# The order of the last store and the x loads of a tile on SyncE's queue, in a residual add with RMSNorm on one core

## The chip, the cores and the metric

The kernel runs on one core of one Trainium2 chip. The metric is device microseconds (us) of that core, from one execution of the whole kernel. Three runs of the kernel before took 4003.17, 4016.13 and 4017.06 us; their median, 4016.13, is the time before.

## The reference

The inputs are x and residual, both 32 x 2048 x 2048 in fp32, and gamma, 2048 numbers in fp32. Each of the 65,536 rows is treated alone:

```
z   = x + residual
rms = sqrt(mean(z ** 2, axis=-1) + eps)
out = z / rms * gamma
```

So 1073.7 MB are read and 536.9 MB are written, whatever the order of the work.

## The kernel before, in words

**Tiles.** The rows are cut into 65 tiles. Tile 0 has 3 rows in each of the 128 partitions, tiles 1 to 63 have 8, tile 64 has 5. A full tile is 8.39 MB of x, as much of residual, as much of output. The tile's x goes into one of two buffers, z[0] and z[1], by the tile's parity, and everything is done there in place: VectorE adds residual to it, scales it, and the stores read it. So the buffer that held tile i-1 takes x of tile i+1, and a load of x may begin only where the store has finished. Residual goes into one area of 9 rows (`r_area`), which neighbouring tiles share, shifted by one row: residual of tile i+1 is loaded once the first two of the three adds of tile i are done.

**Groups.** The store of a tile and the x load into the same buffer are cut into four groups, q = 0 to 3, each of every fourth partition (q, q+4, ...): 32 partitions, 2.10 MB in a full tile. Each group's store counts on a semaphore of its own (`s_out[q]`), and the x load of the same group waits for that. In this text S0 to S3 are the four stores of a tile (helper `store`, line 170) and L0 to L3 the four loads of x into the same partitions (helper `load_x`, line 149).

**Engines and queues.** SyncE (SP in the profile, SPq its DMA queue, q1) issues all stores and all loads of x, in the order of `sync_program` and `sp_turn`, which is written out by hand: one call of `sp_turn(sp, i)` for i = 1 to 63. It waits until VectorE has finished tile i-1 (semaphore `done`), stores tile i-1, and loads x of tile i+1. An instruction of SP that waits for a semaphore holds up all that stand behind it on SP. ScalarE (ACT) issues the loads of residual from its own queue (ACTq, line 161, q10), in `act_turn`, between its sums of squares. VectorE (DVE) runs `dve_turn`: it waits for all four x loads (`x_in`) and for residual (`r_in`), adds in three parts (line 195), then per half a reciprocal (line 219) and one scaling per row (line 200), the roots coming from ACT (line 256). At the end of the second half it raises `done`. TensorE does nothing.

**The turn before.** `sp_turn` queues S0, S1, S2 of tile i-1, then L0, L1, L2 of tile i+1, each after its group's store has landed, then S3, then L3, which waits until S3 has landed.

**Head and tail.** Tiles 0 and 1 are loaded whole, and gamma is spread over the partitions meanwhile. The last tiles are stored by rows (line 175): tile 63 in two halves, tile 64 in three pieces.

Of the kernel before, what the change touches and what calls it, by code (L numbers as in the profile page):

```python
# [9 lines left out]
def kernel(  # L10
# [32 lines left out]
    Q = 4  # L43
# [16 lines left out]
    def rows(t, i):  # L60
        k = sizes[i]
        return t[starts[i] : starts[i] + P * k, :].rearrange("(p r) m -> p r m", r=k)
# [82 lines left out]
    def group(q):  # L145
        return slice(q, P, Q)

    def load_x(sp, i, q):
        sp.dma_start(out=z[i % 2][group(q), : sizes[i], :], in_=rows(x_f, i)[group(q)]).then_inc(  # L149
            ev["x_in"][i % 2], U  # L150
        )
# [17 lines left out]
    def store(sp, i, q):  # L169
        sp.dma_start(out=rows(o_f, i)[group(q)], in_=z[i % 2][group(q), : sizes[i], :]).then_inc(  # L170
            s_out[q], U
        )
# [4 lines left out]
    def sp_turn(sp, i):  # L177


        def load(q):  # L180
            sp.wait_ge(s_out[q], i * U)
            load_x(sp, i + 1, q)

        Turn(i).wait(sp, "done", -1)
        for q in range(Q - 1):
            store(sp, i - 1, q)
        for q in range(Q - 1):
            load(q)
        store(sp, i - 1, Q - 1)
        load(Q - 1)  # L190


    def add(v, i, a, b):
# [92 lines left out]
    def sync_program(sp):  # L286
        whole_x(sp, 0)
        load_r(sp, Turn(0))

        sp.wait_ge(tail_ev["add"], 1)  # L290
        for q in range(4):
            sp.dma_start(  # L292
                out=stage[32 * q : 32 * q + 1],
                in_=gamma.partition_broadcast(1).rearrange("p (a b) -> p a b", a=16),
            ).then_inc(g_in, U)
        load_r(sp, Turn(1))
        whole_x(sp, 1)
        for i in range(1, last):
            sp_turn(sp, i)
        (a0, b0), (a1, b1) = halves(last - 1)  # L300
        sp.wait_ge(half, 1)
        store_rows(sp, last - 1, a0, b0)
        Turn(last).wait(sp, "done", -1)
        store_rows(sp, last - 1, a1, b1)
        for k, (a, b) in enumerate(tail):
            sp.wait_ge(tail_ev["done"], k + 1)
            store_rows(sp, last, a, b)
# [94 lines left out]
```

## Time and profile before

| | |
|---|---|
| median of three runs | 4016.13 us (4003.17 to 4017.06) |
| the profiled execution, its own time | 3982.87 us |
| its span | 3981.1 us (1.77 us lie around it) |
| DVE busy | 2300.7 us, 58% of the span |
| ACT busy | 1059.7 us, 27% |
| HBM read, written | 1073.77 MB, 536.87 MB; mean 405 GB/s over the span |

The busy time of an engine is the sum of its instructions, without the issuing of DMAs. A DMA queue's share is the time that its packets took, summed over the core's 16 DMA engines, as a share of 16 spans. In a table of stretches (windows), a packet is booked in the stretch in which it starts, with all of its time: so the DMA share of a short stretch can be above 1, and share divided by GB/s tells how long the DMA engines took per byte there. In a timeline a row's first number is its start in us from the span's start, the second its length, and in brackets stands how long the engine had been idle and what ended that. The length of a DMA instruction on SP or ACT is that of its issue, not of the transfer.

### The profile page before, as it was taken

Reading aid. Unit: us, or ns where it says so; the run is one execution under the profiler, and the core shown is the slowest. Engines: PE = TensorE matmul, PEld = TensorE weight load, DVE = VectorE, ACT = ScalarE, POOL = GpSimd, SP = SyncE. Lnnn points to the kernel's source line nnn. Section 1 sums busy time; section 2 is a strip of 40 time slices with the busy share of each in tenths; the row PEclk is TensorE's granted clock in tenths of the full one; section 3 lists DMA queues with packets and bytes.
Section 4 is the critical chain, followed back from the end, with each engine's and each line's share of the span. In section 5 each row is a group of like instructions: output and inputs, shape, how many; then the busy total and the mean of one; then the engine's idle time right before and its main releaser. Section 6 shows DMA issues by size and latency. Waiting matters only on the chain.

```text
span 3981.1 us, 4005 instructions
## 1 busy us (share of the span) xinstructions
DVE 2300.7 (58%) x842; ACT 1059.7 (27%) x1157; POOL 0.2 (0%) x4
## 2 busy tenths in 40 slices
DVE  5646556465564655646556465564655646556465
ACT  2313223132231322313223132231322313223132
POOL 0000000000000000000000000000000000000000
DMA  9999999999999999999999999999999999999999
GB/s 421 411 392 420 399 402 410 390 415 396 400 411 400 411 400 408 403 400 412 400 409 402 400 411 400 400 411 400 413 398 411 411 400 411 400 400 410 390 421 379
DMA packets 34694, 1610.73 MB, mean 405 GB/s; under 512 B 9280, under 2 KB 9344, under 8 KB 9344
## 3 DMA queue, kind: packets, MB, share of 16 engines
q1 hardware_dynamic: 25616, 1085.34, 65.9%
q10 hardware_dynamic: 9072, 525.34, 30.5%
q14 instruction: 6, 0.05, 0.0%
HBM read 1073.77 MB, written 536.87 MB: 405 GB/s over the span
## 4 chain that ended last, share of the span: by engine, by line
DMA 94%; SPq 3%; DVE 1%; issue 1%; another core or an unknown queue 1%; ACT 0%; ACTq 0%; DVEq 0%
DMA out_dram<-z 93%; SPq L170 2%; SPq L149 1%; DVE z L200 1%; DVE z L195 1%; DMA z<-in_gamma_dram 0%; DMA z<-in_x_dram 0%; ACT sq_junk L246 0%; SPq L292 0%; DVE z L311 0%; ACT rms L256 0%; DVE rstd L219 0%; ACTq L161 0%; DVE tail_rstd L329 0%
## 5 line engine op out<-in xcount | busy, mean ns | idle before, releaser
L195 DVE TENSOR_TENSOR z<-z,r_area 128x8192 f32<-128x8192 f32 (+2 forms) x192 | 1104.8, 5809 | 1589.9 <-DMA z<-in_x_dram 1579.0
L246 ACT ACTIVATE sq_junk<-z 128x2048 f32<-128x2048 f32 x512 | 962.1, 1879 | 2891.2 <-DVE z L195 2880.9
L200 DVE SCALAR_TENSOR_TENSOR z<-z,rstd,gamma_tile 128x2048 f32<-128x2048 f32 x507 | 1156.5, 2343 | 4.5
L246 ACT ACTIVATION_READ_ACCUMULATOR sq_junk<-z 128x1 f32 x512 | 95.4, 186 | 0.0
L219 DVE RECIPROCAL rstd<-rms 128x4 f32<-128x4 f32 (+1 forms) x128 | 22.3, 174 | 58.2 <-ACT rms L256 58.2
L256 ACT ACTIVATE rms<-ssq,eps_tile 128x4 f32<-128x4 f32 (+1 forms) x128 | 38.0, 297 | 11.7
L200 DVE SCALAR_TENSOR_TENSOR z<-z,tail_rstd,gamma_tile 128x2048 f32<-128x2048 f32 x5 | 11.6, 2346 | 0.1
L313 DVE LOAD_MASK_SELECT gamma_tile<-z x1 | 0.0, 14 | 16.3 <-DMA z<-in_gamma_dram 16.3
L195 DVE TENSOR_TENSOR z<-z 128x2048 f32<-128x2048 f32 x3 | 6.7, 2284 | 0.0
L313 DVE STREAM_SHUFFLE gamma_tile<-z 128x2048 f32<-128x2048 f32 x1 | 2.3, 2290 | 0.0
L311 DVE MEMSET z<- 128x2048 f32 x1 | 1.8, 1765 | 0.4 <-issue 0.4
L246 ACT ACT_TABLE_LOAD x1 | 1.3, 1283 | 0.9 <-SPq L80 0.9
L256 ACT ACT_TABLE_LOAD x1 | 1.3, 1283 | 0.1
L256 ACT ACTIVATE tail_rms<-tail_ssq,eps_tile 128x2 f32<-128x2 f32 (+1 forms) x3 | 0.9, 295 | 0.1
L310 DVE MEMSET eps_tile<- 128x1 f32 x1 | 0.1, 59 | 1.0 <-SPq L80 1.0
L329 DVE RECIPROCAL tail_rstd<-tail_rms 128x2 f32<-128x2 f32 (+1 forms) x3 | 0.5, 158 | 0.0
L383 POOL MEMSET const-bfloat16-1.0<- 128x1 bf16 x1 | 0.1, 101 | 0.0
L383 POOL MEMSET const-uint8-127<- 128x1 uint8 x1 | 0.1, 101 | 0.0
L383 POOL MEMSET const-float32-0.0<- 128x1 f32 x1 | 0.1, 98 | 0.2 <-issue 0.2
L383 POOL MEMSET const-float32-1.0<- 128x1 f32 x1 | 0.1, 98 | 0.0
## 6 DMA issues: line engine op xcount, KB each, us to landing
out_dram<-z SPq DMA_DIRECT2D x2, 4096.0 KB, 20.9
z<-in_x_dram SPq DMA_DIRECT2D x4, 1280.0 KB
r_area<-in_residual_dram ACTq DMA_DIRECT2D x1, 5120.0 KB, 25.6
out_dram<-z SPq DMA_DIRECT2D x2, 2048.0 KB, 8.6
z<-in_x_dram SPq DMA_DIRECT2D x249
out_dram<-z SPq DMA_DIRECT2D x248, 20.6
z<-in_x_dram SPq DMA_DIRECT2D x1, 3072.0 KB
z<-in_residual_dram SPq DMA_DIRECT2D x1, 3072.0 KB, 17.2
```

The lines of the kernel that those rows point to most:

```text
L149: sp.dma_start(out=z[i % 2][group(q), : sizes[i], :], in_=rows(x_f, i)[group(q)]).then_inc(ev["x_in"][i % 2], U)
L170: sp.dma_start(out=rows(o_f, i)[group(q)], in_=z[i % 2][group(q), : sizes[i], :]).then_inc(s_out[q], U)
L195: return v.tensor_add(out=s, in0=s, in1=res(i, a, b))
L200: ins = v.scalar_tensor_tensor(out=s, in0=s, scalar=rs[:, c + g - a : c + g - a + 1], in1=gamma_tile[:, :], op0=mult, op1=mult,)
L219: v.reciprocal(out=rstd[p][h][:, :n], in_=rms[p][h][:, :n]).then_inc(dve, U)
L246: s.activation(out=sq_junk[:, :], in_=src[:, g, :], func=Act.Square, accum_out=sq[:, c + g - a : c + g - a + 1],)
L256: return s.activation(out=rm, in_=sq, func=Act.Sqrt, bias=eps_tile[:, :], scale=inv_d)
L310: v.memset(eps_tile[:, :], float(eps))
L311: v.memset(stage, 0.0).then_inc(tail_ev["add"], 1)
L313: v.stream_shuffle(gamma_tile[:, :].rearrange("p (a b) -> p a b", a=16), stage, [0] * 32)
L329: v.reciprocal(out=tail_rstd[:, a:b], in_=tail_rms[:, a:b]).then_inc(dve, U)
L383: nc = _bacc.Bacc("TRN2", target_bir_lowering=False, num_devices=1)
```

## The change

Within `sp_turn`, all four stores of tile i-1 are queued first, and then the four loads of x of tile i+1, each still waiting for the store of its own group. Before, the last store stood between the loads of the third and the fourth group. No wait is added or removed, and the other engines' programs are the same, with line numbers behind the place lower by two.

```diff
         Turn(i).wait(sp, "done", -1)
-        for q in range(Q - 1):
+        for q in range(Q):
             store(sp, i - 1, q)
-        for q in range(Q - 1):
+        for q in range(Q):
             load(q)
-        store(sp, i - 1, Q - 1)
-        load(Q - 1)
```

One turn on SP in the program before, of a tile in buffer z0 (out_0_dram is the output, in_x_dram is x; x2 stands for two such instructions in a row; the last row begins the next turn, of buffer z1):

```order
L170 DMA out_0_dram<-z0 32x16384 [waits done0]
L170 DMA out_0_dram<-z0 32x16384 x2
L149 DMA z0<-in_x_dram 32x16384 [waits s_out0]
L149 DMA z0<-in_x_dram 32x16384 [waits s_out1]
L149 DMA z0<-in_x_dram 32x16384 [waits s_out2]
L170 DMA out_0_dram<-z0 32x16384
L149 DMA z0<-in_x_dram 32x16384 [waits s_out3]
L170 DMA out_0_dram<-z1 32x16384 [waits done1]
```

The sixth row is S3, directly ahead of L3, which waits for it. The same turn on SP in the changed program:

```order
L170 DMA out_0_dram<-z0 32x16384 [waits done0]
L170 DMA out_0_dram<-z0 32x16384 x3
L149 DMA z0<-in_x_dram 32x16384 [waits s_out0]
L149 DMA z0<-in_x_dram 32x16384 [waits s_out1]
L149 DMA z0<-in_x_dram 32x16384 [waits s_out2]
L149 DMA z0<-in_x_dram 32x16384 [waits s_out3]
L170 DMA out_0_dram<-z1 32x16384 [waits done1]
```

S3 has moved past the three loads L0 to L2 and past their three waits; the loads keep their order among themselves and L3 is still the last of the turn.

## The prediction

> **What bounds the kernel now.** I read the page first: its last-ended chain and the share of its DMA queues.
>
> ```profile
> span 3981.1 us, 4005 instructions
> ...
> DMA packets 34694, 1610.73 MB, mean 405 GB/s; under 512 B 9280, under 2 KB 9344, under 8 KB 9344
> ## 3 DMA queue, kind: packets, MB, share of 16 engines
> q1 hardware_dynamic: 25616, 1085.34, 65.9%
> q10 hardware_dynamic: 9072, 525.34, 30.5%
> ...
> DMA 94%; SPq 3%; DVE 1%; issue 1%; another core or an unknown queue 1%; ACT 0%; ACTq 0%; DVEq 0%
> ```
>
> The chain is DMA for 94%, so compute hides. The two queues' packets take 65.9 + 30.5 = 96.4% of the DMA engines' time, so the engines stand idle for 3.6% of 3981.1 us: 143 us, or 2.27 us in each of the 63 turns, if it falls on the turns alike. Small as that looks, it must be found: then it must be asked whether the 96.4% are all full speed.
>
> Next, SP's timeline over one turn in the middle:
>
> ```profile
> 2026.19 0.47 SPq L149 DMA_DIRECT2D z<-in_x_dram  x1
> 2026.71 1.87 SPq L170 DMA_DIRECT2D out_dram<-z  x3
> 2039.76 10.35 SPq L149 DMA_DIRECT2D z<-in_x_dram  x3
> 2050.14 0.60 SPq L170 DMA_DIRECT2D out_dram<-z  x1
> 2088.22 0.47 SPq L149 DMA_DIRECT2D z<-in_x_dram  x1
> ```
>
> The first row is L3 of a turn, issued when S3 had landed; then S0 to S2 of the next tile, L0 to L2 as each store lands, and S3 at 2050.14. L3 comes only at 2088.22, 38.1 us later, because S3 stands behind L1 and L2 and shares the engines with residual. From L3 to L3 the turn takes 62.03 us. ACT's residual load and VectorE's work in that turn, with the median time to landing of the residual loads from the DMA view as the last row:
>
> ```profile
> 2035.10 17.36 DVE L195 TENSOR_TENSOR z<-z,r_area 128x8192 f32<-128x8192 f32 x3 [25.18 <-DMA z<-in_x_dram]
> 2050.44 0.34 ACTq L161 DMA_DIRECT2D r_area<-in_residual_dram  x1
> 2053.60 9.12 DVE L200 SCALAR_TENSOR_TENSOR z<-z,rstd,gamma_tile 128x2048 f32<-128x2048 f32 x4
> 2062.85 9.12 DVE L200 SCALAR_TENSOR_TENSOR z<-z,rstd,gamma_tile 128x2048 f32<-128x2048 f32 x4
> ...
> r_area<-in_residual_dram ACTq DMA_DIRECT2D x62, 37.9
> ```
>
> Residual, issued at 2050.44, lands about 37.9 us later, at 2088.3: in the same moment as S3. So when S3 lands, nothing else is queued anywhere: not residual, not x, and not the next tile's stores, which have been ready since 2062.85 + 9.12 = 2071.97 but stand behind L3 on SP. Both queues run dry once per turn. The table of stretches shows it, with two stretches of the head for comparison (the last two numbers of a row are DMA share and GB/s):
>
> ```profile
> 30.00:52.00 22.00, 5.68 (x4) 2.04 (x3) 0.00 (x0) 1.00 1.00 432
> 62.10:72.90 10.80, 10.80 (x2) 6.01 (x6) 0.00 (x0) 1.00 1.09 467
> 2023.70:2027.40 3.70, 0.00 (x0) 0.00 (x0) 0.00 (x0) 1.00 0.00 0
> 2027.40:2033.80 6.40, 0.00 (x0) 0.00 (x0) 0.00 (x0) 1.00 1.03 328
> 2033.80:2048.40 14.60, 13.30 (x2) 4.43 (x5) 0.00 (x0) 1.00 1.00 431
> 2048.40:2085.80 37.40, 22.58 (x12) 12.08 (x14) 0.00 (x0) 1.00 1.04 449
> ```
>
> Third row: for 3.7 us no packet starts; L3's begin 1.2 us after its issue. Fourth row: L3 alone. Its packets take 1.03/328 = 0.00314 of the engines' time per GB/s, against 1.00/432 = 0.00231 in the head: 1.36 times as long. Fifth and sixth: S0 to S2 alone, then the loads and S3 beside residual, at 1.00/431 and 1.04/449, full speed again. So a turn loses twice: an empty queue, and a first load behind it that runs slowly.
>
> **The change part by part.** It moves one instruction per turn, S3, in 63 turns, with its 2.10 MB, on SP and on q1, past the three loads L0 to L2 and their waits. It is not moved past anything of ACT's queue, and VectorE's and ACT's programs are untouched. Bytes and issue times are the same: S3's 0.60 us is paid right behind S2's, while q1 has work.
>
> What it removes. S3 runs directly behind S2, and lands about one group's time (2.10 MB at 432 GB/s: 4.85 us) after it. Then L3 is issued while L0 to L2 are still queued. SP then waits for `done`. In the quoted turn, counted from the add's start at 2035.10 (x complete), S0 to S3 end about 4 x 4.85 = 19.4 us later, and so L3 is issued at about +20 us; VectorE finishes the tile at +36.9 (2071.97 - 2035.10). At +36.9 the next four stores go into q1, behind what is left of L0 to L3, which ends with the turn at about +58. So 21 us of cover stand between the stores' issue and an empty q1. If that cover were gone, each us of lateness would cost one us per turn.
>
> What a turn then costs. It moves 3 x 8.39 = 25.17 MB. At 432 GB/s, the head's rate, that is 58.25 us. What it takes now is read from the adds: the second tile's, then the first and last of 61 that follow each other, and the last tile's:
>
> ```profile
> 105.76 17.36 DVE L195 TENSOR_TENSOR z<-z,r_area 128x8192 f32<-128x8192 f32 x3 [10.96 <-DMA r_area<-in_residual_dram]
> ...
> 168.17 17.36 DVE L195 TENSOR_TENSOR z<-z,r_area 128x8192 f32<-128x8192 f32 x3 [25.53 <-DMA z<-in_x_dram]
> ...
> 3900.40 17.36 DVE L195 TENSOR_TENSOR z<-z,r_area 128x8192 f32<-128x8192 f32 x3 [25.59 <-DMA z<-in_x_dram]
> ...
> 3948.35 10.96 DVE L195 TENSOR_TENSOR z<-z,r_area 128x4096 f32<-128x4096 f32 x3 [12.04 <-DMA z<-in_x_dram]
> ```
>
> (3900.40 - 168.17) / 60 = 62.20 us per turn. So 62.20 - 58.25 = 3.95 us per turn can go. The two losses account for it: L3 alone takes 0.36 x 4.85 = 1.73 us too long, the empty queue the remaining 2.2, which agrees with the 2.27 of the page.
>
> The sum. 60 turns x 3.95 = 237 us. The last turn goes from 3900.40 to 3948.35 in 47.95 us and moves 8.39 + 2 x 5.24 = 18.87 MB, 43.7 us at 432 GB/s: 4.3 us more. The turn from 105.76 to 168.17 (62.41 us) is like the sixty: 4 us. The one ahead of it I take at nothing: its stores are those of the small tile 0, and its end waits for residual (first row), not for x. Behind the last add nothing changes: 3981.1 - 3948.35 = 32.75 us, set by the adds, roots and scalings of tile 64 and their stores, while tile 63's stores run beside them. So the span falls by 245 us to 3736. As a check, all 1610.73 MB at 432 GB/s are 3729 us, and a few us of head and tail come on top.
>
> Not all will go. The mean turn is 62.20 where the quoted one is 62.03; what makes some turns longer by 0.17 on the mean I can't place, so I keep it: 62 x 0.17 = 11 us. Another unknown is the change from load to store: in the quoted turn L3 is the only load directly ahead of a store without residual beside it, and it is slow. That a load behind others, with no empty queue ahead, is fast is shown by the second row: L0 to L2 of the second turn, groups of 32 partitions and no residual yet, at 1.09/467 = 0.00233. The bounds are 0 and 1.73 us per turn; I take 0, being nearest to that row. Span 3736 + 11 = 3747, own time 3747 + 1.8 = 3749 us.
>
> The median of the three runs is 33 us (0.8%) above the profiled execution. If this stretches every turn alike, the new median is 3749 x 1.0083 = 3780; if it lies in the empty queues and slow loads, it goes with them and 3749 stays. I take the middle, **3764 us**, with 3730 to 3795 as this case's own range.
>
> The rate 432 GB/s carries the sum. The Trainium skill (DMA: Bandwidth & Descriptors, Bandwidth: Measured) gives 425 GB/s for a 16 MB load by one core. By that figure a turn would take 59.2 us, an estimate, and the median would come out near 3825; this case's own rows hold 432 over 22 us, so they decide.
>
> Who is late next? Residual: issued 15.3 us after the add begins (2050.44 - 2035.10), landing 37.9 later, at +53.2, against +58 for x: 5 us of slack. It shares the engines with three groups, as before (L1, L2, S3 then; L0 to L2 now), so I leave 37.9. VectorE's chain of 36.9 us fits in 58.
>
> **The rivals.**
>
> *L3 stays slow.* Perhaps not the empty queue makes it slow, but what it is: the last group, alone, with a store behind it. All that would still hold. Then only the 2.2 us of emptiness go, and 62 x 1.73 = 107 us come back: own time 3856, median 3856 to 3888. Against it stands the second row of the stretches; for it, that every slow L3 has a store behind it and that row's loads mostly a load. A load of a group reads rows 256 KB apart, in all DMA engines at once. The Trainium skill (DMA: Bandwidth & Descriptors, Latency and other measured facts) reports DMA copies at 207 GB/s where the rows of the partitions lie 512 KiB apart, and infers that streams in step meet in the same memory channel; by that L3 is slow by its addresses wherever it stands in step. The trace agrees only where a queue starts empty: 328 GB/s at 1.03 there, full speed with the same addresses at 62.1. I give 0.17.
>
> *The gap moves.* The queues could run dry somewhere else: if S0 to S3 were queued only after L3 had ended, the empty time would come back between L3 and S0, and the time would stay within 20 us of 4016. By the rows `done` comes 21 us before that; it would need VectorE's 36.9 us to become 58. Chance 0.04.
>
> *Slower: residual beside loads only.* In the new order residual runs beside L0 to L2, three loads; before, beside L1, L2 and S3. If reading alone from both queues slowed the engines, the 8.39 + 3 x 2.10 = 14.7 MB, 34 us at full speed, would stretch. From 12% on (3.95/34) the gain is gone; at L3's 1.36 times it is 12.2 us per turn, 8.3 net, and the median 4016 + 62 x 8.3 = 4530. Against it: the sixth row, where residual and loads share for most of 37 us, at full speed (1.04/449 = 0.00232), and the first, loads alone. Chance 0.04.
>
> **How the numbers follow.** The forecast has the remaining 0.75. A measurement of this kernel can tell about 0.5%, 20 us, from no change. Faster: 0.75 + 0.17 = 0.92; within 0.5%: 0.04; slower: 0.04. The range starts at 3728 (all bytes at 432 GB/s) and must go into the first rival to leave out no more than 2 in 10: to 3872, the middle of its 3856 to 3888.
>
> **What would show it.** Right: both DMA queues together near 99% of the engines' time, mean near 430 GB/s; add to add 58.3 to 58.6 us; in SP's timeline four stores in a row some 37 us after the add begins and L3 20 us after it, no row in which SP waits 38 us for a store; no stretch of 3 us without packets, and L3's stretch at a share over GB/s of 0.0023. If that quotient is 0.0031 there and the turn 60, the first rival is right. Wrong: a turn of 62 us with a new empty stretch, or adds that end their wait on residual rather than on x.

## The result, and the profile after

The changed kernel takes 3732.51 us (median of four runs, 3732.22 to 3733.14), the kernel before 4010.93 us (four runs, the three from above among them, 4003.17 to 4017.06). The ratio is 0.9307, with a 95% interval of 0.9287 to 0.9327: 7% faster.

The page of the changed kernel, the rows that answer to those of before:

```profile
span 3730.9 us, 4005 instructions
...
DMA packets 34695, 1610.73 MB, mean 432 GB/s; under 512 B 9281, under 2 KB 9345, under 8 KB 9345
## 3 DMA queue, kind: packets, MB, share of 16 engines
q1 hardware_dynamic: 25616, 1085.34, 67.3%
q10 hardware_dynamic: 9072, 525.34, 32.6%
...
DMA 65%; DVE 27%; issue 5%; SPq 1%; ACT 1%; another core or an unknown queue 1%; ACTq 0%; DVEq 0%
```

The DMA engines are now at work for 67.3 + 32.6 = 99.9% of the span. Two products tell where the time went. Work: 0.964 x 3981.1 = 3838 us before, 0.999 x 3730.9 = 3727 us now, for the same bytes, so the packets took 111 us less. Idleness: 143 us before, 4 us now, 139 us less. Together 250 us, the whole difference of the spans. The chain of waits now runs through VectorE for 27% of the span, and that is a trap for a reader: stores wait for `done` and the chain follows that wait, but while SP waits there, the queue still holds loads. An engine that stands in the chain is not yet a bound; the DMA engines' 99.9% say what is.

SP's timeline over one turn, then VectorE's add and ACT's residual load of the same turn, and the two adds that bound sixty turns with the last tile's add behind:

```profile
1944.51 2.42 SPq L170 DMA_DIRECT2D out_dram<-z  x4
1970.49 17.48 SPq L149 DMA_DIRECT2D z<-in_x_dram  x4
2002.68 2.41 SPq L170 DMA_DIRECT2D out_dram<-z  x4
...
1965.79 17.36 DVE L193 TENSOR_TENSOR z<-z,r_area 128x8192 f32<-128x8192 f32 x3 [21.30 <-DMA z<-in_x_dram]
1981.12 0.34 ACTq L161 DMA_DIRECT2D r_area<-in_residual_dram  x1
...
164.31 17.36 DVE L193 TENSOR_TENSOR z<-z,r_area 128x8192 f32<-128x8192 f32 x3 [17.30 <-DMA z<-in_x_dram]
...
3653.80 17.36 DVE L193 TENSOR_TENSOR z<-z,r_area 128x8192 f32<-128x8192 f32 x3 [21.38 <-DMA z<-in_x_dram]
...
3698.09 10.96 DVE L193 TENSOR_TENSOR z<-z,r_area 128x4096 f32<-128x4096 f32 x3 [8.39 <-DMA z<-in_x_dram]
```

The four stores go out at 2002.68, 36.9 us after the add began; the last of the four loads at 1970.49 + 17.48 = 1987.97, 22.2 us after it. A turn takes (3653.80 - 164.31) / 60 = 58.16 us, against 62.20. The table of stretches shows what became of the gap and of L3; the middle row holds L3, between residual's end and the next stores:

```profile
1928.00:1957.00 29.00, 16.45 (x9) 6.03 (x7) 0.00 (x0) 1.00 1.00 434
1957.00:1963.00 6.00, 0.00 (x0) 0.00 (x0) 0.00 (x0) 1.00 0.91 393
1963.00:1984.00 21.00, 17.36 (x3) 8.34 (x10) 0.00 (x0) 1.00 1.02 443
```

There is no stretch without packets, and L3 runs at 0.91/393 = 0.0023, where it stood at 0.0031.

### The profile page after: what moved, and what is told of

Read it like the earlier page. It is cut to its first block, busy times and chain, and to the rows that moved or that the text cites. A ratio compares the mean times of both kernels' runs of the same rounds, so it can differ in the third digit from the quotient of the medians.

```text
span 3730.9 us, 4005 instructions
## 1 busy us (share of the span) xinstructions
DVE 2300.7 (62%) x842; ACT 1059.7 (28%) x1157; POOL 0.2 (0%) x4
## 3 DMA queue, kind: packets, MB, share of 16 engines
q1 hardware_dynamic: 25616, 1085.34, 67.3%
q10 hardware_dynamic: 9072, 525.34, 32.6%
## 4 chain that ended last, share of the span: by engine, by line
DMA 65%; DVE 27%; issue 5%; SPq 1%; ACT 1%; another core or an unknown queue 1%; ACTq 0%; DVEq 0%
DMA out_dram<-z 33%; DMA z<-in_x_dram 30%; DVE z L193 13%; DVE z L198 13%; SPq L170 1%; DMA r_area<-in_residual_dram 1%; ACT sq_junk L244 0%; DMA z<-in_gamma_dram 0%; ACTq L161 0%; DVE rstd L217 0%; ACT rms L254 0%; DVEq L314 0%; DVEq L139 0%; SPq L290 0%
```

## The experiments

The theory on trial: a turn lost time only because both queues ran empty when S3 landed, and because what follows such a gap starts slowly. The rival that was left: it is S3's place that counts, what runs beside residual, or what stands beside what. All kernels compute the whole output. From each profile I work out, as above, the idle time of the DMA engines (span less busy) and the excess of the packets (busy less the 3727 us of the changed kernel); a share has one decimal, so both are good to some 4 us. The profiled execution can lie above the median of its runs, by 10 us with stores and loads in turn and by 8 with S3 one load earlier. Each ratio is to runs of the kernel before beside those of the row (medians 3999 to 4011 us); small differences between rows are best read from the ratios.

| kernel | median us | ratio to before (95%) | idle us | excess us |
|---|---|---|---|---|
| before (profile) | 4010.93 | 1 | 143 | 111 |
| changed | 3732.51 | 0.9307 (0.9287 to 0.9327) | 4 | 0 |
| S3 one load earlier | 3742.12 | 0.9354 (0.9338 to 0.9369) | 0 | 21 |
| order of before, L3 from ACT | 3745.78 | 0.9362 (0.9344 to 0.9380) | 4 | 12 |
| gap ahead of the stores | 3896.86 | 0.9744 (0.9728 to 0.9761) | 113 | 55 |
| gap between loads | 3974.44 | 0.9930 (0.9913 to 0.9946) | 143 | 106 |
| wait for S3, residual queued | 3835.46 | 0.9587 (0.9564 to 0.9609) | 19 | 86 |
| wait for S2, residual queued | 3783.60 | 0.9446 (0.9426 to 0.9466) | 4 | 55 |
| stores and loads in turn | 3818.92 | 0.9539 (0.9523 to 0.9555) | 4 | 97 |
| L0 alone between stores | 3841.30 | 0.9590 (0.9574 to 0.9606) | 12 | 105 |
| two groups, order of before | 4296.35 (one run) | | 253 | 314 |

**How much of the move is needed.** S3 is moved past one load only.

```diff
         for q in range(Q - 1):
             store(sp, i - 1, q)
-        for q in range(Q - 1):
+        for q in range(Q - 2):
             load(q)
         store(sp, i - 1, Q - 1)
-        load(Q - 1)
+        for q in range(Q - 2, Q):
+            load(q)
```

> S3 is moved past one load only: S0 S1 S2 L0 L1 S3 L2 L3. Theory (a turn loses time only where both queues are empty, and then by the slow load behind the gap): when S3 lands, L2 is still queued, so nothing runs empty and the time is that of the changed kernel, 3732 us, within 15. Rival (what pays is that S3 no longer runs beside residual, in favour of a load): S3 still runs beside residual, so 3950 to 4011. A middle time, 3800 to 3900, would say that one group of 2.1 MB is too little cover.

3742.12 us: as the theory had it. S3 still runs beside residual, and nearly all of the gain is there. One group queued behind S3 is cover enough to keep the queues from running empty. What is left to the changed kernel, 10 us between the medians, is excess of the packets (21 us in the profiled execution), not idleness.

**The order of before, without SP being held up.** S3 stays behind L2, and L3 still waits for it, but on ScalarE's queue, after the turn's last root.

```diff
         store(sp, i - 1, Q - 1)
-        load(Q - 1)
...
         inc(root(s, chain, ssq[p][1][:, :n], rms[p][1][:, :n]), "rms_b", i)
+        if i:
+            s.wait_ge(s_out[Q - 1], i * U if t.it is None else t.it * U + i * U)
+            src = rows(x_f, i + 1) if t.it is None else x_full[t.it + i]
+            s.dma_start(
+                out=z[(i + 1) % 2][group(Q - 1), : sizes[i + 1], :], in_=src[group(Q - 1)]
+            ).then_inc(ev["x_in"][(i + 1) % 2], U)
```

> The order of before, S3 as late as there and L3 still waiting for it, but L3 is issued from ScalarE's queue at the end of its turn, so that SP goes on to the next tile's stores as soon as they are ready. Theory: when S3 lands, S0 to S2 of the next tile are queued, the engines never run empty: 3732 to 3770 us (some turns longer, since L3 now shares with S0 and x is complete up to 5 us later). Rival (the place of S3 itself matters, behind the loads and beside residual): 4011.

3745.78 us. So the place of S3 is not the cause. What cost the time was that L3's wait for S3 kept the next tile's finished stores, which stand behind it on SP, out of the queue. SP's waits (us in total, times, longest) show it. Before:

```profile
SPq L149 <- DMA out_dram<-z: 3612.7, 252, 38.2
SPq L170 <- DVE z L200: 33.6, 2, 30.1
```

With L3 issued from ScalarE, where the stores' line is L172, and then the queues of this kernel's page:

```profile
SPq L172 <- DVE z L201: 1892.3, 63, 31.3
...
q1 hardware_dynamic: 22592, 954.00, 59.1%
q10 hardware_dynamic: 12096, 656.68, 40.8%
```

Before, SP came late to the stores in all but two cases, since the tile was finished when it arrived there. Now it waits for VectorE in every turn, so the stores go out as soon as they can, and the DMA engines are at work for 99.9% of the span.

**The gap given back, ahead of stores.** The changed kernel with one more wait: the stores are queued only when x of the running tile has landed.

```diff
+        Turn(i).wait(sp, "x_in")
         Turn(i).wait(sp, "done", -1)
         for q in range(Q):
             store(sp, i - 1, q)
```

> The changed kernel with one more wait: SP queues S0 to S3 only when x of the running tile has landed, so both queues are empty once per turn, ahead of a store instead of a load. Theory: the empty time comes back, 63 x 2.2 = 139, but not the slow load, since a store stands behind the gap: 3871 us, and S0's stretch at a share over GB/s of 0.0023. If whatever stands first behind a gap is slow, 63 x 3.95 = 249 comes back: 3981, S0 at 0.0031. If emptiness costs nothing and only S3's place counts: 3732.

3896.86 us, 26 us more than the theory's 3871 and far from the other two. The idle time comes back, 113 us or 1.8 per turn. The table of stretches of this kernel, from the gap to residual's start:

```profile
1987.60:1990.10 2.50, 0.00 (x0) 0.00 (x0) 0.00 (x0) 1.00 0.00 0
1990.10:2006.60 16.50, 16.04 (x3) 6.26 (x7) 0.00 (x0) 1.00 1.03 445
2006.60:2009.00 2.40, 1.48 (x2) 2.31 (x4) 0.00 (x0) 1.00 1.32 437
```

Stores behind a gap are at full speed at once (1.03/445 = 0.0023). But an excess of 55 us, 0.9 per turn, appears where nobody had looked for it: in the third row, the last packets of S3, directly ahead of residual's load, at 1.32/437 = 0.0030.

**The gap given back, between loads.** L3 is issued only when L0 to L2 have landed, which is when residual lands too.

```diff
-        for q in range(Q):
+        for q in range(Q - 1):
             load(q)
+        sp.wait_ge(ev["x_in"][(i + 1) % 2], Turn(i).at(1, Q * U) - U)
+        load(Q - 1)
```

> The changed kernel with one more wait: L3 is issued only when L0 to L2 have landed, which is when residual lands too, so both queues run empty once per turn as in the kernel before, and L3 stands alone behind the gap, but behind loads and not behind a store. Theory A (a load behind an empty queue is slow): gap and both of L3's packets come back, 63 x 3.95, about 3981 us, L3's first packets at 3.2 us against 2.4. Theory B (only the change between storing and loading, in step, is slow): gap and the packet ahead of the next store come back, 63 x (2.2 + 1.0), about 3930 us.

3974.44 us: theory A, within 7 us. Idle time and excess are those of the kernel before (143 and 106 us, against 143 and 111), though no store has anything to do with this gap. The queues of its page, and its stretches (gap, L3, the stores behind it):

```profile
q1 hardware_dynamic: 25616, 1085.34, 65.9%
q10 hardware_dynamic: 9072, 525.34, 30.5%
...
1957.60:1961.30 3.70, 0.00 (x0) 0.00 (x0) 0.00 (x0) 1.00 0.00 0
1961.30:1966.80 5.50, 0.00 (x0) 0.00 (x0) 0.00 (x0) 1.00 1.19 381
1966.80:1988.00 21.20, 17.99 (x5) 9.07 (x10) 0.00 (x0) 1.00 1.03 445
```

L3, alone behind the gap and with stores behind it, stands at 1.19/381 = 0.0031 again.

**A wait on S3 without a gap.** SP issues the loads only when S3 has landed; residual is queued on the other queue by then.

```diff
         for q in range(Q):
             store(sp, i - 1, q)
+        sp.wait_ge(s_out[Q - 1], i * U)
         for q in range(Q):
             load(q)
```

> The changed kernel with one more wait: SP issues L0 only when S3 has landed, so q1 is empty once per turn between S3 and L0, at a time when residual has been queued for some us on the other queue. Theory (only a gap on both queues together costs): 3732 to 3750 us. Rival (every landing that the queue waits for costs its 2.2 us, or 3.95 with the slow load): 3871 or 3981.

3835.46 us: neither. One half of the theory holds: residual covers the empty SP queue, and the idle time is only 19 us in place of 143. The other half falls: 86 us of excess are there without a gap. The page and the stretches of this kernel (stores; the change to residual; residual and loads; the end of L3 with S0 behind it):

```profile
span 3832.4 us, 4068 instructions
...
q1 hardware_dynamic: 25616, 1085.34, 67.0%
q10 hardware_dynamic: 9072, 525.34, 32.5%
```

```profile
1960.00:1979.00 19.00, 15.94 (x3) 6.16 (x7) 0.00 (x0) 1.00 1.00 431
1979.00:1982.00 3.00, 2.04 (x3) 2.91 (x4) 0.00 (x0) 1.00 1.07 393
1982.50:2013.00 30.50, 17.39 (x9) 6.94 (x9) 0.00 (x0) 1.00 1.02 440
2015.50:2018.30 2.80, 0.00 (x0) 0.00 (x0) 0.00 (x0) 1.00 1.34 421
```

Full speed in the first and third (0.0023), 0.0027 where storing turns to loading, 0.0032 where loading turns to storing. Against 432 GB/s the second row lost 3.0 x (1.07 - 393/432) = 0.5 us and the fourth 2.8 x (1.34 - 421/432) = 1.0 us of this turn, so about two thirds of the excess stand at the end of L3. The slow packets need no gap.

**Which packets of a lone load are slow.** Two groups instead of four in the kernel before, so that a group has four packets per DMA engine.

```diff
-    Q = 4
+    Q = 2
```

> The order of before with two groups instead of four: S0, L0 after S0, S1, L1 after S1, four packets for each DMA engine in a group. The queue now runs empty twice per turn, ahead of L0 and of L1. Theory A (whatever load stands alone behind an empty queue is slow throughout): L1's stretch of about 13 us at a share over GB/s of 0.0031 all along, 9.6 us lost per turn, about 4340 us. Theory B (only packets next to a change between storing and loading, with the DMA engines in step, are slow): first and last quarter of L1 at 0.0031, the middle at 0.0023, 7 us lost per turn, about 4170 us.

4296.35 us in one run, nearer to A, but the stretches show B's pattern in L1, which is issued at 1974.50:

```profile
1974.80:1978.50 3.70, 0.00 (x0) 0.00 (x0) 0.00 (x0) 1.00 0.86 283
1978.50:1982.00 3.50, 0.00 (x0) 0.00 (x0) 0.00 (x0) 1.00 1.30 562
1982.00:1988.00 6.00, 0.00 (x0) 0.00 (x0) 0.00 (x0) 1.00 0.96 317
```

0.0030, 0.0023, 0.0030: the beginning, behind the gap, and the end, ahead of the stores, are slow, the middle is not. With the gap between loads this fits two causes, one for each end of L3: its first packets are slow as a load behind a gap (a gap behind loads did it too), its last because stores follow. The second is read from the place of the slow packets alone; no kernel was run in which nothing follows such a load.

**Does the order matter where nothing runs empty?** The changed kernel's stores and loads in turn, S0 S1 L0 S2 L1 S3 L2 L3:

```diff
-        for q in range(Q):
-            store(sp, i - 1, q)
-        for q in range(Q):
-            load(q)
+        store(sp, i - 1, 0)
+        for q in range(1, Q):
+            store(sp, i - 1, q)
+            load(q - 1)
+        load(Q - 1)
```

> The changed kernel's stores and loads in turn: S0 S1 L0 S2 L1 S3 L2 L3. The queue always holds at least one group when a load is issued. Theory (the order is free as long as nothing runs empty): 3732 us, within 15. If having all four stores together, far from the loads, matters in itself: over 3760.

3818.92 us, a miss: no idle time (4 us), and 97 us of excess. The stretches of this kernel, with residual running and around L0 ahead of it:

```profile
1975.00:2005.00 30.00, 17.53 (x9) 7.08 (x9) 0.00 (x0) 1.00 1.03 448
2020.30:2028.00 7.70, 7.70 (x2) 3.81 (x3) 0.00 (x0) 1.00 0.98 340
```

0.0029 around L0, 0.0023 where the other changes stand, beside residual.

**One load between stores.** L0 alone is put between S1 and S2.

```diff
-        for q in range(Q):
-            store(sp, i - 1, q)
-        for q in range(Q):
-            load(q)
+        store(sp, i - 1, 0)
+        store(sp, i - 1, 1)
+        load(0)
+        store(sp, i - 1, 2)
+        store(sp, i - 1, 3)
+        for q in range(1, Q):
+            load(q)
```

> The changed kernel with L0 alone moved between the stores: S0 S1 L0 S2 S3 L1 L2 L3. In the interleaved order the slow packets stood around L0, before residual starts, and L1 beside residual was at full speed. If a load between stores costs only while no residual runs beside it, this order costs as much as the interleaved one: about 3819 us, within 20. If the number of changes between storing and loading counts, wherever they stand, it costs about half of that: about 3775 us. If neither, 3732 us.

3841.30 us, 2 us outside the first answer's range: one load of 2.1 MB between stores costs as much as the whole order in turn. Its stretches (S0 and S1, L0 with S2, residual with the loads):

```profile
1960.00:1971.50 11.50, 5.73 (x1) 0.00 (x0) 0.00 (x0) 1.00 0.99 427
1971.50:1979.30 7.80, 7.80 (x2) 4.66 (x5) 0.00 (x0) 1.00 1.07 370
1984.00:2013.00 29.00, 18.51 (x10) 8.15 (x9) 0.00 (x0) 1.00 1.00 434
```

**A milder wait.** As the wait on S3, but on S2, with S3 still queued:

```diff
+        sp.wait_ge(s_out[Q - 2], i * U)
         for q in range(Q):
             load(q)
```

> The changed kernel with one more wait, milder than the one ahead of the loads in an earlier run (3835 us): SP issues L0 to L3 only when S2 has landed, with S3 still queued for 4.85 us. Theory (a wait on all 16 engines brings them into step, and changes between loading and storing in step are slow): with one group of cover the engines need not stop for each other, 3735 to 3780 us. If 3835 us comes back, the issue of four loads at once is slow by itself, whatever the cover.

3783.60 us, 4 us above the range given, and half-way between the changed kernel (3732.5) and the wait on S3 (3835.5). The excess is 55 us, in the change from L3 to S0:

```profile
1960.00:1988.00 28.00, 13.91 (x8) 3.52 (x5) 0.00 (x0) 1.00 1.02 440
1988.50:1993.80 5.30, 0.00 (x0) 0.00 (x0) 0.00 (x0) 1.00 1.01 383
```

0.0023 ahead of it, 0.0026 in it. The same change from L3 to S0, with no gap ahead of it, stands at 0.0023 in the changed kernel, 0.0026 here, 0.0032 with the wait on S3. How far the 16 DMA engines have drifted apart goes with it in part: in the trace's records of semaphore landings, the parts of S0 from the 16 engines land within 0.7 us (median over the turns) in the kernel before, 2.6 us in the two kernels with a wait, 6.1 us in the changed one. That fits the idea that engines in step are slow at the change. But it is a correlation, and it leaves much unexplained: the two waits differ (0.0026 and 0.0032) at the same spread, L0 between stores is slow at a spread of 3.4 us, and the stores behind a gap are fast at a spread of 0.2 us. Why a change is slow stays open.

## Why the prediction was right, and where it was not

**What bounds the kernel, and the two losses.** Right, and in size: 2.2 us of emptiness and 1.73 us of a slow L3 per turn were forecast, and 139 / 63 = 2.2 and 111 / 63 = 1.8 went. A kernel without the move (L3 from ACT) and one with the least of it (S3 one load earlier) show that it was the emptying, and two more bring the emptiness back; of these, the gap between loads brings back the slow L3 as well.

**The turn.** 58.25 us plus 0.17 kept; measured 58.16. SP's steps came as worked out: stores at +36.9 us, L3 at +22 (forecast +20). The 21 us of cover held: the stores are queued at +37, and x, the last of what stood ahead of them, is complete at +58.

**The sum.** Sixty turns gave 3732.23 - 3489.49 = 243 us (237 forecast). The last turn, 3698.09 - 3653.80 = 44.29, gave 3.7 (4.3 forecast); the end behind it is the same, 32.81 us. The first turns were misjudged. Of the kernel before, the add of tile 1; that of tile 2, at 105.76, was shown:

```profile
57.88 17.36 DVE L195 TENSOR_TENSOR z<-z,r_area 128x8192 f32<-128x8192 f32 x3 [20.84 <-DMA z<-in_x_dram]
```

The same two adds after:

```profile
58.45 17.36 DVE L193 TENSOR_TENSOR z<-z,r_area 128x8192 f32<-128x8192 f32 x3 [21.52 <-DMA z<-in_x_dram]
...
110.14 17.36 DVE L193 TENSOR_TENSOR z<-z,r_area 128x8192 f32<-128x8192 f32 x3 [14.76 <-DMA r_area<-in_residual_dram]
```

The turn that I took at nothing became 110.14 - 58.45 = 51.69 us in place of 47.88, because its end waits for residual. By the trace's packet records residual ran beside the small store S3 and L3 before; now its first packet starts 1.8 us later (78.5 us in place of 76.6), and it runs beside L3 and S0 of the next tile. The turn behind it then took 54.17 in place of 62.41. Together they gave 4.4 us, against 4 forecast: the two errors cancel.

**The 31 us that the forecast was too high.** 3764 against 3732.5. Three terms were mis-sized, all to the same side, by some 11, 15 and 6 us. The 11 us for what makes some turns longer fell away: the runs now lie within 0.9 us, where those of before spread over 14. Of the 33 us between the profiled execution of before and the median I kept half; nothing of it stayed, for the profiled execution after took 3732.66, in the middle of its runs. So both went with the order of before and not with the chip's rate. What in that order makes them isn't shown: the runs with the gap ahead of the stores lie within 0.7 us, with 113 us of idleness, and those with S3 one load earlier spread over 13 us with none. And 432 GB/s was a little low: a turn's 25.17 MB in 58.16 us are 433. The Trainium skill's 425 GB/s (DMA: Bandwidth & Descriptors, Bandwidth: Measured), by which the median was to be near 3825, does not hold for this mix: 432 over 3730.9 us.

**The rival "L3 stays slow".** It did not, in this order; its chance of 0.17 was not too high, though. Its reasoning, that a load with a store behind it is slow whether or not a gap is ahead, came true in part in the wait on S3 (some two thirds of 86 us, against its 107), and a change of loading and storing alone cost 97 to 105 us in two other orders. My reason for setting it aside, loads of groups at full speed in the second turn, was no good test: no store of a full tile stood behind them. So the 0 us that the sum puts for a slow L3 came out right, but the reason given, no empty queue ahead, does not suffice, and there was luck in it. What saved the forecast is that the changed kernel's engines pass from loading to storing once per turn, and, for a reason only partly shown, at no cost. The Trainium skill's inference for slow strided copies, streams in step meeting in one memory channel (DMA: Bandwidth & Descriptors, Latency and other measured facts), fits the spread of the engines above only as far as that goes: not L0 between stores, nor the fast stores behind a gap. No run here looked at a memory channel.

**The other rivals.** The gap did not move, and residual beside loads only runs at full speed (1.00/434 in the first row of the stretches after).

## What to carry to other kernels

Where DMA engines are busy "9" in all slices, work out two numbers, the share that is missing and the time per byte: queues that ran empty for 2.2 us in each turn came with nearly as much again, 1.8 us, of slow packets. A wait for a transfer's landing must not stand ahead of finished work on the same issuing engine. It is cheaper where another transfer is still queued, but not free: L3's wait for S3 cost 10 us with a load of 2.1 MB still queued, while a wait ahead of all four loads cost 51 us with S3 still queued, and 103 us with residual alone.

Mixing loads and stores can cost time while the DMA engines are hardly ever idle: a single load between stores, before residual ran, cost 109 us of 3732, with the DMA engines 99.7% busy. A single store between loads, beside residual, cost 10 us. So the place has to be measured, and not only the number of changes.

## What the runs showed of the hardware

- A change from loading to storing or back can slow the packets beside it with no queue empty: 0.0026 to 0.0032 in place of 0.0023 (share over GB/s). In the orders with four groups, the stretches shown in the midst of residual's load on the other queue were at full speed (1.00/434 to 1.04/449), changes included.
- A load of a group behind an empty queue is slow whether a store or loads stood ahead of the gap (0.0031); stores behind one are not (0.0023).
- While the other queue had work, an empty queue left the DMA engines idle for 19 us in all, in place of 143; the slow packets at the changes were there all the same (86 us).
- The 16 DMA engines moved 432 GB/s over the whole span, at 99.9% busy, with two bytes read for one written, and no order that was tried was faster.
